# Six gate weights of the last branch staged in the pool of activations' buffers

## The chip, the cores and the metric

The kernel runs on one core of one Trainium2 chip. The metric is the device time of one execution in microseconds (us), the median of several runs.

## What is computed

A trunk of two encoder layers over 512 positions of width 1024, all in float32:

```python
h = _rms_norm(x, ln1_g[l])
proj = jnp.einsum('bsd,dn->bsn', h, w_in[l])
(a_q, a_k, a_v, b_q, b_k, b_v, c_cq, c_ckv, c_kr, gate_logits) = _split_columns(proj)
y_a = _gqa_axial(...); y_b = _diff_attention(...); y_c = _mla(...)
y = jnp.stack([y_a, y_b, y_c], axis=2)
gates = jax.nn.sigmoid(gate_logits.reshape(b, s, N_BRANCH, d))
merged = jnp.sum(gates * jnp.einsum('bsne,ned->bsnd', y, w_branch[l]), axis=2)
x = x + jnp.einsum('bsd,de->bse', merged, w_out[l])
h2 = _rms_norm(x, ln2_g[l])
x = x + jnp.einsum('bsf,fd->bsd', jnp.square(jax.nn.relu(h2 @ w_ff1[l])), w_ff2[l])
```

Three attentions with 8 heads each (A, B, C) run from the same normalised input. Each is projected to width 1024 and weighted by its own gate. The change touches the gate of the third branch, C (the latent attention).

## The kernel before

**Weights.** Each weight is loaded as a raw float32 tile `wr` by a DMA that SP's queue issues, and is then split into two parts for TensorE: ACT copies it to a rounded `wh` (line 61), and POOL (in the attention stages) or DVE (elsewhere, gate 7 included) takes the rest into `wl` (line 67). POOL does this in pieces of 256 columns. A matmul of a weight against a split activation is three matmuls per block of 128 rows: `wh` against the high part, `wh` against the low part, `wl` against the high part. The raw tiles share one pool tag, "wr", of only two buffers; `wh` and `wl` have three each. A raw buffer is free again when both `wh` and `wl` have been made from it.

**Activations.** Nearly all activations (queries `c_Q`, keys `c_K`, values, outputs `ya`/`yb`/`yc`, gate values `gc`) are tiles of 4 KB per partition and share another tag, "s4", of 25 buffers. A raw gate weight, 128 x 1024 float32, has the same size.

**Order.** A plan lists steps with estimated costs. `weave` mixes the steps of an attention (scores of a head and a block of 128 queries) with fill steps (projections, gates). Fetches and splits are called some microseconds of planned time ahead of their step. The framework's scheduler then takes every instruction with its place in that order as priority, hands out pool buffers as they come free, and writes the final order of each engine's instructions; each engine works through its own list in order and waits where an instruction isn't ready. So a pool that has a free buffer earlier or later changes the order on all engines.

**The stage.** Attention C of a layer runs with these fills: with heads 4 and 5, the last query and key projection `c_pair(l, 3)` and gates 0 to 2 of branch C; with heads 6 and 7, gates 3 to 5; after it, gates 6 and 7 and then the eight branch projections `br`. One gate is 24 matmuls (8 blocks of 3). Per unit of attention, PE does scores `sc` (3 matmuls into one of two banks of PSUM), DVE a maximum `mx`, ACT the exponential `p` (line 602), DVE the normalisation `p` (line 607), PE four transposes `pT` (line 613), ACT and DVE the split `pt` (lines 616, 617), and PE for each pair of units eight matmuls `pv`. `c_pair` gives two queries (`c_Q`, lines 228 and 233) and two keys (`c_K`), each finished by copies that SP's queue issues (line 238). The final part of a head goes by `fx`, `yt` and `yc` (lines 626, 627, 228).

**Names.** Of layer 0, the raw tiles of the eight gates of branch C are, in order, `wr_5501`, `wr_5652`, `wr_5728`, `wr_5814`, `wr_5914`, `wr_6007` (the six of the change, called gate 0 to 5 here) and `wr_6091`, `wr_6120` (gates 6 and 7). The tiles split from gates 0, 1 and 2 are `wh_5565`, `wh_5654`, `wh_5730`. Layer 1 has the same rows under other numbers.

Of the kernel before, what the change touches and what calls it, by code (L numbers as in the profile page):

```python
# [10 lines left out]
F32 = mybir.dt.float32  # L11
# [31 lines left out]
class Weight:  # L43
# [5 lines left out]
    def fetch(self):  # L49
        if self.raw is None:  # L50
            t = self.t
            self.raw = t.p.tile([128, self.cols], F32, tag=self.tag, name="wr", bufs=t.NWR if self.tag == "wr" else 4)
            t.nc.sync.dma_start(self.raw, self.src)

    def get(self):
# [86 lines left out]
class Trunk:  # L142
# [836 lines left out]
    def gate_branch(self, l, n, d):  # L979

        nc = self.nc
        wg = self.big(l, P_GATE + n * 8 + d)
        wb = self.big(l, P_BR + n * 4 + d // 2, (d % 2) * 512, 512)
        st = {}

        def gate():
            ps = self.ps("L", "gate")
            self.mm(ps, self.fm_pairs(wg, 0, self.xg))
            if n < 2:
                t = self.tmp("gz")  # L990
            else:
                if d % 2 == 0:
                    self.gc[d // 2] = self.s4("gc", dtype=F32)
                t = self.gc[d // 2][:, d % 2]
            st["t"] = t
            nc.vector.tensor_tensor(t, ps, self.rbc, op=ALU.mult)
            nc.scalar.activation(t, t, AF.Tanh, scale=0.5)

        def branch():
            t = st["t"]  # L1000
            ps = self.ps("L", "br")
            self.mm(ps, self.fm_pairs(wb, 0, [self.want(self.ys["abc"[n]], j) for j in range(4)]))
            if n == 0:
                if d % 2 == 0:
                    self.mg[d // 2] = self.s4("mg", dtype=F32)
                nc.vector.scalar_tensor_tensor(self.mg[d // 2][:, d % 2], t, 1.0, ps, op0=ALU.add, op1=ALU.mult)
            else:
                nc.vector.scalar_tensor_tensor(t, t, 1.0, ps, op0=ALU.add, op1=ALU.mult)
                m = self.mg[d // 2][:, d % 2]
                (self.pool if n == 1 else nc.vector.tensor_tensor)(m, m, t, op=ALU.add)  # L1010
                if n == 2:
                    self.mp[d] = self.s4("mp")
                    self.split(self.mp[d], m, 0.5)

        return [(24 * 0.216, gate, [wg]), (12 * 0.216, branch, [wb])]
# [373 lines left out]
```

## Time and profile before

| | |
|---|---|
| time, median of 3 runs | 1870.81 us (1870.26 to 1872.25) |
| profiled execution, its own time | 1866.2 us |
| span of that execution, first to last instruction | 1864.4 us |
| PE busy | 1817.5 us, 97% of the span |
| PE weight loads, beside it | 1599.2 us, 86% |
| DVE busy | 1371.9 us, 74% |
| ACT busy | 1005.0 us, 54% |
| POOL busy | 458.9 us, 25% |
| mean granted TensorE clock | 0.996 |

An engine's busy time over the span says how much room the others have. PE is idle for 46.9 us of the span. Timeline rows give the start, the duration, engine, line and operation, the tiles (out <- in, without buffer numbers), and in brackets how long the engine stood idle ahead of it and what released it. The stage of the change lies at about 434 to 523 us in layer 0 and 919.7 us later in layer 1.

### The profile page before, as it was taken

The numbers are of one execution on the slowest core, as the hardware profiler recorded it, in microseconds if no ns is written. First come the engines' busy times: TensorE is split into PE (matmuls) and PEld (weight loads), VectorE is DVE, ScalarE is ACT, GpSimd is POOL, SyncE is SP. The second block draws the span as 40 slices with busy tenths as digits, with TensorE's granted clock in tenths as the row PEclk, the third lists the DMA queues.
The fourth block names the chain that finished last, engine by engine and source line by source line (L and its number), as shares of the span: only waits on it lengthen the run. The fifth ranks groups of instructions, "written<-read, shape, count | busy, mean of one in ns | idle before, by whom it ended". The sixth has DMA issues, their size and how long they took to land.

```text
span 1864.4 us, 30102 instructions
## 1 busy us (share of the span) xinstructions
PE 1817.5 (97%) x10960; PEld 1599.2 (86%) x10960; DVE 1371.9 (74%) x2812; ACT 1005.0 (54%) x1844; POOL 458.9 (25%) x602
## 2 busy tenths in 40 slices
PE   7999999999999999999999999999999999999997
PEld 7998878787888898988999988787878888989897
DVE  7788889755665776767887888896566667777677
ACT  5477666655543544444445766665554444444443
POOL 4321443454101010101232224434540001001011
PEclk9999999999999999999999999999999999999999
DMA  5413341332153373645534134313232435637363
GB/s 164 115 51 85 97 109 48 97 84 81 52 170 102 92 178 107 156 130 128 153 114 122 41 92 120 90 49 87 81 93 65 168 91 121 166 92 190 102 146 95
DMA packets 87619, 201.45 MB, mean 108 GB/s; under 512 B 12464, under 2 KB 29232, under 8 KB 87472
## 3 DMA queue, kind: packets, MB, share of 16 engines
q1 hardware_dynamic: 77104, 182.75, 33.3%
q0 software_dynamic: 10368, 16.78, 5.9%
q8 instruction: 87, 1.43, 0.3%
q14 instruction: 60, 0.49, 0.1%
HBM read 174.32 MB, written 4.19 MB: 96 GB/s over the span
## 4 chain that ended last, share of the span: by engine, by line
PE 77%; DVE 10%; DMA 5%; ACT 4%; issue 2%; POOL 2%; SPq 0%; DVEq 0%; ACTq 0%; POOLq 0%
PE ff L225 17%; PE ff L1165 13%; PE gate L225 12%; PE br L225 6%; PE tm L317 6%; PE out L225 5%; PE sc L225 4%; PE pv L225 4%; PE pT L613 4%; PE c_rank L225 2%; DMA fa<-wff 2%; DMA fs<-wff 1%; DMA wr<-w 1%; DVE mx L597 1%; DVE p L759 1%
## 5 line engine op out<-in xcount | busy, mean ns | idle before, releaser
L61 ACT CAST wh<-wr 128x1024 fp32r<-128x1024 f32 (+5 forms) x246 | 224.7, 914 | 348.2 <-PE ff L225 114.0
L67 POOL TENSOR_TENSOR wl<-wr,wh 128x256 fp32r<-128x256 f32 (+1 forms) x382 | 281.3, 766 | 513.6 <-ACT wh L61 496.7
L1165 PE MATMUL ff<-h,fh 128*128 128x256 f32 x1792 | 324.6, 284 | 1.5 <-DVE x L1173 1.4
L225 PE MATMUL ff<-xg,wh 128*128 128x512 f32 x1024 | 315.8, 390 | 0.0
L1165 PEld LDWEIGHTS ff<-h,fh 128*128 128x128 f32 x1792 | 278.8, 192 | 3.7 <-issue 2.0
L1165 PE MATMUL ff<-h,fl 128*128 128x256 f32 x896 | 254.1, 285 | 2.3 <-DVE fl L116 2.0
L225 PE MATMUL gate<-xg,wh 128*128 128x512 f32 x768 | 241.9, 393 | 1.1 <-DVE c_K L233 1.1
L225 PEld LDWEIGHTS ff<-xg,wh 128*128 128x128 f32 x1024 | 191.7, 188 | 39.3
L115 ACT CAST fh<-fa 128x640 fp32r<-128x640 f32 (+1 forms) x144 | 108.7, 762 | 178.6 <-PE ff L1165 92.5
L317 PE MATMUL tm<-wh,xg 128*128 128x256 f32 x1024 | 203.0, 290 | 0.0
L597 DVE TENSOR_REDUCE mx<-sc 128x1 f32<-128x512 f32 x256 | 173.6, 683 | 35.2 <-PE sc L225 34.2
L225 PE MATMUL ff<-xg,wl 128*128 128x512 f32 x512 | 199.2, 389 | 0.0
L1165 PEld LDWEIGHTS ff<-h,fl 128*128 128x128 f32 x896 | 171.0, 192 | 5.8 <-DVE fl L116 5.3
L225 PEld LDWEIGHTS gate<-xg,wh 128*128 128x128 f32 x768 | 143.1, 189 | 29.9 <-PE pv L225 1.4
L317 PEld LDWEIGHTS tm<-wh,xg 128*128 128x128 f32 x1024 | 165.1, 192 | 0.2
L67 DVE TENSOR_TENSOR wl<-wr,wh 128x1024 fp32r<-128x1024 f32 (+3 forms) x122 | 140.1, 1149 | 25.5 <-ACT wh L61 25.4
L116 DVE TENSOR_TENSOR fl<-fa,fh 128x640 fp32r<-128x640 f32 (+1 forms) x144 | 126.2, 880 | 38.4 <-ACT fh L115 35.2
L225 PE MATMUL gate<-xg,wl 128*128 128x512 f32 x384 | 150.6, 392 | 0.0
L616 ACT CAST pt<-pT 128x512 fp32r<-128x512 f32 x192 | 111.8, 585 | 65.0 <-PE pT L613 63.5
L617 DVE TENSOR_TENSOR pt<-pT,pt 128x512 fp32r<-128x512 f32 x192 | 131.2, 685 | 19.5 <-ACT pt L616 18.1
L317 PE MATMUL tm<-wl,xg 128*128 128x256 f32 x512 | 145.4, 284 | 0.0
L613 PE MATMUL pT<-ident,p 128*128 128x128 f32 x768 | 115.8, 274 | 11.0 <-DVE p L607 5.4
(253 smaller groups left out, 3491.2 us busy)
## 6 DMA issues: line engine op xcount, KB each, us to landing
wr<-w SPq DMA_DIRECT2D x170, 512.0 KB, 3.6
fa<-wff SPq DMA_DIRECT2D x64, 320.0 KB, 3.5
wr<-w SPq DMA_DIRECT2D x52, 256.0 KB, 2.9
fa<-wff SPq DMA_DIRECT2D x32, 384.0 KB, 3.8
b_sq<-b_f SPq DMA_DIRECT2D x96, 64.0 KB, 2.7
b_sk<-b_f SPq DMA_DIRECT2D x96, 64.0 KB, 2.0
fa<-wff POOLq DMA_DIRECT2D x16, 320.0 KB, 5.2
fs<-wff SPq DMA_DIRECT2D x32, 160.0 KB, 2.8
```

Of the source, the lines that this page charges most:

```text
L61: t.nc.scalar.copy(wh, self.raw)
L67: e.tensor_tensor(wl[:, q], self.raw[:, q], wh[:, q].bitcast(F32), op=ALU.subtract)
L115: t.nc.scalar.copy(a, x)
L116: t.nc.vector.tensor_tensor(b, x, a.bitcast(F32), op=ALU.subtract)
L225: self.nc.tensor.matmul(out, l, r, start=(i == 0), stop=(i == n - 1))
L317: self.nc.tensor.matmul(ps, l, r, start=(u == 0 and i == 0 and tt % 2 == 0), stop=(u == 1 and tt % 2 == 1 and i == len(p) - 1))
L597: nc.vector.tensor_reduce(m, s, axis=AX.X, op=ALU.max, negate=True)
L613: nc.tensor.transpose(T[:, k], p[:, k * 128 : (k + 1) * 128], self.ident)
L616: nc.scalar.copy(h[:, :, q], T)
L617: nc.vector.tensor_tensor(lo[:, :, q], T, h[:, :, q].bitcast(F32), op=ALU.subtract)
L759: nc.vector.scalar_tensor_tensor(p0, p1, z1, p0, op0=ALU.mult, op1=ALU.add)
L1165: nc.tensor.matmul(bk[tag], x, y, start=(new and a == 0), stop=(part[1] == n and a == len(pairs) - 1), skip_group_check=True)
```

## The change

The raw tiles of gates 0 to 5 of branch C (`n == 2 and d < 6`) carry the tag "s4" in place of "wr", so they come out of the 25 buffers of activations. The number of "s4" buffers stays 25.

```diff
@@ class Weight, fetch @@
-            self.raw = t.p.tile([128, self.cols], F32, tag=self.tag, name="wr", bufs=t.NWR if self.tag == "wr" else 4)
+            self.raw = t.p.tile([128, self.cols], F32, tag=self.tag, name="wr", bufs={"wr": t.NWR, "s4": t.NS4, "pt": 4}[self.tag])
@@ Trunk.gate_branch @@
         wg = self.big(l, P_GATE + n * 8 + d)
+        if n == 2 and d < 6:
+
+            wg.tag = "s4"
         wb = self.big(l, P_BR + n * 4 + d // 2, (d % 2) * 512, 512)
```

Instructions, tiles and bytes are the same in both kernels; only their order and their buffers differ, and only in this stage, in both layers alike. SP's queue before, from the raw tile of gate 0 on (`c_Q_5537`, `c_Q_5543` are the last two queries, `c_K_5579`, `c_K_5584` the last two keys):

```order
L53 DMA wr_5501<-w1024 128x1024
L53 DMA wr_5652<-w1024 128x1024
L238 DMA c_Q_5537<-c_qr_4395 32x512 x2
L53 DMA wr_5728<-w1024 128x1024
L238 DMA c_Q_5543<-c_qr_4395 32x512 x2
L53 DMA wr_5814<-w1024 128x1024
L238 DMA c_K_5579<-c_krf_3505 64x512
L238 DMA c_K_5584<-c_krf_3505 64x512
L53 DMA wr_5914<-w1024 128x1024
L53 DMA wr_6007<-w1024 128x1024
L53 DMA wr_6091<-w1024 128x1024
L53 DMA wr_6120<-w1024 128x1024
```

The same place of SP's queue in the changed kernel:

```order
L53 DMA wr_6091<-w1024 128x1024
L53 DMA wr_6120<-w1024 128x1024
L53 DMA wr_5501<-w1024 128x1024
L238 DMA c_Q_5537<-c_qr_4395 32x512 x2
L238 DMA c_Q_5543<-c_qr_4395 32x512 x2
L238 DMA c_K_5579<-c_krf_3505 64x512
L238 DMA c_K_5584<-c_krf_3505 64x512
L53 DMA wr_5652<-w1024 128x1024
L53 DMA wr_5728<-w1024 128x1024
L53 DMA wr_5814<-w1024 128x1024
L53 DMA wr_5914<-w1024 128x1024
L53 DMA wr_6007<-w1024 128x1024
```

Gates 6 and 7 now take the two "wr" buffers first and keep them; gate 0's raw tile stands third, in the buffer (and with the wait: the scores `sc_5471`) that `c_Q_5537` had before; the copies of `c_Q` and `c_K` are no longer parted by weights; and gates 1 to 5 come behind them. Gate 1's raw tile takes the buffer of gate 0's, once that has been split. The others take buffers that this stage's `c_pair` leaves.

ACT's list before, from the cast of gate 0 on:

```order
L61 CAST wh_5565<-wr_5501 128x1024
L616 CAST pt_5453<-pT_5520 128x4x128
L602 ACTIVATE p_5514,z_5515<-sc_5508,mx_5512,c_rq_4065 128x512
L61 CAST wh_5654<-wr_5652 128x1024
L228 ACTIVATE c_Q_5537<-uq_5527 64x512 x2
L602 ACTIVATE p_5559,z_5560<-sc_5553,mx_5557,c_rq_4065 128x512
L61 CAST wh_5730<-wr_5728 128x1024
L228 ACTIVATE c_Q_5543<-uq_5527 64x512 x2
L228 ACTIVATE c_K_5579<-uk_5572 64x512 x2
L616 CAST pt_5589<-pT_5591 128x4x128
L602 ACTIVATE p_5604,z_5605<-sc_5598,mx_5602,c_rq_4065 128x512
L228 ACTIVATE c_K_5584<-uk_5572 64x512 x2
```

ACT's list in the changed kernel, from the third row of that piece on:

```order
L602 ACTIVATE p_5514,z_5515<-sc_5508,mx_5512,c_rq_4065 128x512
L228 ACTIVATE c_Q_5537<-uq_5527 64x512 x2
L228 ACTIVATE c_Q_5543<-uq_5527 64x512 x2
L602 ACTIVATE p_5559,z_5560<-sc_5553,mx_5557,c_rq_4065 128x512
L228 ACTIVATE c_K_5579<-uk_5572 64x512 x2
L616 CAST pt_5589<-pT_5591 128x4x128
L602 ACTIVATE p_5604,z_5605<-sc_5598,mx_5602,c_rq_4065 128x512
L228 ACTIVATE c_K_5584<-uk_5572 64x512 x2
L626 COPY fx_5618<-pv_5462 64x512
L228 ACTIVATE yc_5621<-yt_5370 128x512
L616 CAST pt_5589<-pT_5661 128x4x128
L1000 ACTIVATE gc_5649<-gc_5649 128x512
```

The casts of gates 1 and 2 (`wh_5654`, `wh_5730`) have left this piece; they now stand three and five rows behind its end. The cast of gate 0 stays where it was.

On PE the piece between gate 0 and gate 1, as a difference (unmarked and "+" rows are the changed kernel's):

```order
 L225 MATMUL sc<-c_K,c_Q 128x512 x2
 L225 MATMUL sc<-krl,c_Q 128x512
+L225 MATMUL pv<-pt,c_V 128x256 x8
+L225 MATMUL sc<-c_K,c_Q 128x512 x2
+L225 MATMUL sc<-krl,c_Q 128x512
+L613 MATMUL pT<-ident,p 128x128 x3
 L225 MATMUL gate<-xg_97,wh 128x512 x2
 L225 MATMUL gate<-xg_97,wl 128x512
```

Before, gate 1 followed the scores `sc_5677` and `sc_5689` at once; now `pv_5744`, the scores `sc_5762` and three transposes of `p_5683` (the exponential of `sc_5677`) stand ahead of it. Ahead of gate 3 the eight matmuls `pv_5930`, and ahead of gate 5 one `pv`, have moved up in the same way.

## The prediction

> **What bounds the kernel now.** I read the page's head, then TensorE's waits in the two stretches that the change touches, then the engines' rows in order of time there.
>
> ```profile
> span 1864.4 us, 30102 instructions
> PE 1817.5 (97%) x10960; PEld 1599.2 (86%) x10960; DVE 1371.9 (74%) x2812; ACT 1005.0 (54%) x1844; POOL 458.9 (25%) x602
> ```
>
> PE is the bound: a change that leaves its instructions alone can gain only from its idle time, 46.9 us in all. The waits of PE from 440 to 530 us (columns: who waited for whom, total, times, longest) are one row, and from 1360 to 1450 us, the same stage in layer 1, the answer is the same row:
>
> ```profile
> PE pT L613 <- DVE p L607: 2.5, 1, 2.5
> ```
>
> So at stake here is one stall per layer. Around it, PE's rows (start, duration; the last is layer 1's):
>
> ```profile
> 449.06 0.60 PE L613 MATMUL pT<-ident,p 128*128 128x128 f32 x4
> ...
> 450.19 1.08 PE L225 MATMUL pv<-pt,c_V 128*128 128x256 f32 x8
> 451.11 0.63 PE L225 MATMUL gate<-xg,wh 128*128 128x512 f32 x2
> ...
> 456.57 0.60 PE L613 MATMUL pT<-ident,p 128*128 128x128 f32 x4
> 459.65 0.63 PE L613 MATMUL pT<-ident,p 128*128 128x128 f32 x4 [2.49 <-DVE p L607]
> ...
> 1379.29 0.63 PE L613 MATMUL pT<-ident,p 128*128 128x128 f32 x4 [2.45 <-DVE p L607]
> ```
>
> After gate 0 (451.11 to 456.57) PE waits for the normalised `p_5604`. ACT's rows say why, with the last SP row of a weight ahead of them and its landing:
>
> ```profile
> 441.28 1.18 SPq L238 DMA_DIRECT2D c_Q<-c_qr  x2
> 449.41 0.33 SPq L53 DMA_DIRECT2D wr<-w  x1
> DMA to landing us min/median/max: 4.5/4.5/4.5
> 443.83 1.05 ACT L61 CAST wh<-wr 128x1024 fp32r<-128x1024 f32 x1 [0.22 <-issue]
> 445.14 0.59 ACT L616 CAST pt<-pT 128x512 fp32r<-128x512 f32 x1 [0.26 <-PE pT L613]
> 445.81 0.78 ACT L602 ACTIVATE p<-sc,mx,c_rq 128x512 f32<-128x512 f32 x1
> ...
> 448.07 1.07 ACT L228 ACTIVATE c_Q<-uq 64x512 fp32r<-64x512 f32 x2
> 449.03 0.76 ACT L602 ACTIVATE p<-sc,mx,c_rq 128x512 f32<-128x512 f32 x1
> ...
> 454.04 1.05 ACT L61 CAST wh<-wr 128x1024 fp32r<-128x1024 f32 x1 [4.15 <-DMA wr<-w]
> 455.12 1.08 ACT L228 ACTIVATE c_Q<-uq 64x512 fp32r<-64x512 f32 x2
> 456.22 1.19 ACT L228 ACTIVATE c_K<-uk 64x512 fp32r<-64x512 f32 x2
> 457.44 0.58 ACT L616 CAST pt<-pT 128x512 fp32r<-128x512 f32 x1
> 457.92 0.78 ACT L602 ACTIVATE p<-sc,mx,c_rq 128x512 f32<-128x512 f32 x1
> ...
> 460.04 0.58 ACT L626 COPY fx<-pv 64x512 f32<-64x512 f32 x1
> 461.38 0.63 ACT L228 ACTIVATE yc<-yt 128x512 fp32r<-128x512 f32 x1 [0.76 <-DVE yt L627]
> ```
>
> ACT stands 4.15 us before the cast of gate 2's raw tile: issued at 449.41, when a "wr" buffer came free, it lands 4.5 us later. Behind that cast wait `c_Q`, `c_K` and the exponential (457.92) that PE's transposes at 459.65 need. After that stall the granted clock (second column from the right but one) falls in layer 0, and doesn't in layer 1:
>
> ```profile
> 460.00:462.00 2.00, 2.00 (x9) 1.59 (x8) 1.92 (x3) 1.21 (x4) 0.00 (x0) 0.63 0.42 170
> 462.00:464.00 2.00, 2.00 (x7) 1.54 (x5) 1.35 (x4) 2.00 (x5) 0.98 (x2) 0.51 0.00 0
> 1380.00:1382.00 2.00, 2.00 (x10) 1.66 (x9) 1.97 (x4) 1.24 (x3) 0.00 (x0) 1.00 0.29 117
> ```
>
> The clock there is 0.63 and 0.51 of full speed: 2 x 0.37 + 2 x 0.49 = 1.7 us lost in layer 0, none in layer 1.
>
> **Removed.** With the casts of gates 1 and 2 out of this piece of ACT's list, the 4.15 us wait is gone, and with it the stalls: -2.49 - 2.45 = -4.9 us. The clock loss of 1.7 us goes with the long gap: -1.7 us.
>
> **Added: gate 0's raw tile comes later.** It was in place when its cast ran at 443.83. Now it is issued where the `c_Q` copies stood, at 441.28. I take 4.5 us to land, the row of the raw tile at 449.41, since that one too had two `c_Q` copies behind it: 445.8. The raw tile of gate 7 is in flight 0.9 us ahead of it. Bounds: 3.6 us (the same size without company, first row below) and 7.9 us (the last of four of this size issued within 2 us, second row).
>
> ```profile
> wr<-w SPq DMA_DIRECT2D x170, 512.0 KB, 3.6
> DMA to landing us min/median/max: 5.0/6.7/7.9
> ```
>
> So ACT's list shifts by 445.85 - 443.83 = 2.0 us at this cast. `p_5514`, two rows on, feeds the transposes at 449.06. Cast to cast start takes 0.95, `pt` 0.48 more: exponential at 447.3 (before: 445.81); from its start to the end of the normalisation takes 1.6 (rows below), 448.9: just in time, cost 0 to 0.3, taken as 0.1.
>
> The nearest unhindered passage from scores to a normalised `p` (PE, DVE, ACT, DVE):
>
> ```profile
> 483.67 0.39 PE L225 MATMUL sc<-krl,c_Q 128*128 128x512 f32 x1
> 484.10 0.69 DVE L597 TENSOR_REDUCE mx<-sc 128x1 f32<-128x512 f32 x1 [0.33 <-PE sc L225]
> 485.08 0.78 ACT L602 ACTIVATE p<-sc,mx,c_rq 128x512 f32<-128x512 f32 x1 [1.18 <-DVE mx L601]
> 486.18 0.48 DVE L607 TENSOR_SCALAR p<-p,z 128x512 f32<-128x512 f32 x1
> ```
>
> From the start of an exponential to the end of its normalisation 486.66 - 485.08 = 1.6; to the end of the exponential 0.8.
>
> **Added: a chain on ACT that ends late.** From `p_5514` (447.3 to 448.15) the list reads, with the durations above: `c_Q` pair 1.07; then DVE's normalisation, maximum and `c_Q` remainder, on which the second pair waits, 0.9; `c_Q` pair 1.07; exponential 0.9; `c_K` pair 1.2; `pt` 0.5; exponential 0.9; `c_K` pair 1.2; `fx` 0.6; DVE's `yt` 0.8; `yc` 0.6. Sum 9.7: `yc` ends at 457.9 (before: 462.0). The two exponentials in it are normalised by 453.3 and 455.3, ahead of the transposes at 456.57 and 457.0. Hence PE runs on without the stall: transposes to 457.45, scores `sc_5677` and `sc_5689` to 458.8. There stands now `pv_5744`, not gate 1. Its second matmul needs DVE's `pt`, which comes after `yc`'s remainder and gate 0's product, three DVE operations of 0.6 from start to start (each 0.7 long) from 457.9: 459.75. PE waits 0.9, and `pv` ends at 460.6. Next `sc_5762` needs its PSUM bank back from `p_5683`: behind that `pt` come DVE's maximum, one more `pt` and a small scaling, 1.4, exponential from 461.2 to 462.0: PE waits 1.4. The transposes wait for the normalisation (462.8, PE is there at 462.65): 0.15. Gate 1's cast is done at 463.1; its third matmul waits for POOL's first piece:
>
> ```profile
> 463.02 2.83 POOL L67 TENSOR_TENSOR wl<-wr,wh 128x256 fp32r<-128x256 f32 x4 [5.05 <-ACT wh L61]
> 488.01 2.82 POOL L67 TENSOR_TENSOR wl<-wr,wh 128x256 fp32r<-128x256 f32 x4 [6.81 <-ACT wh L61]
> ```
>
> A piece is 0.7 and two matmuls cover 0.45: 0.25. Together 2.7 per layer. Ahead of gate 3 and gate 5 the same kind of tight passage costs about 0.2 (the scores amid gate 3 for their bank) and 0.15 (`yt` ahead of `pv`): 0.35. Per layer 0.1 + 2.7 + 0.35 = 3.15; both layers +6.3.
>
> Bounds of this term: below, with ACT and DVE never late, the scores chain alone is left: `mx` start to exponential end is 485.86 - 484.10 = 1.8 and 0.2 from the scores, against 1.6 of PE work (`sc_5689`, `pv`), 0.35, with 0.1 and 0.25 as above: 0.7 per layer. Above, a landing of 7.9 shifts the whole chain by 3.4: 6.5 per layer.
>
> **Costed at nothing.** The copies of `c_Q` and `c_K` keep SP's queue from gate 1 for some 4 us, but gate 1's raw tile waits for POOL to finish gate 0 (about 450) anyway, and five raw tiles at even 2 us each are there before their casts, the first at 462. Gates 6 and 7 hold both "wr" buffers until their casts, near 500 to 505 where POOL's last piece ended at 490.8 before; behind them wait the raw tiles of the branch projections. Their cover:
>
> ```profile
> 523.22 22.09 PE br L225 x96
> wr<-w SPq DMA_DIRECT2D x52, 256.0 KB, 2.9
> ```
>
> The first of them needs 2.9 to land and two passes of 0.7 before 523.2, so there are over 10 us to spare; if that cover were gone, PE would wait at `br`. POOL, at 25%, has one piece of gate 0 moved behind two additions, done before gate 0 starts.
>
> **Sum.** -4.9 - 1.7 + 6.3 = -0.3 us on the profiled execution: 1866.2 goes to 1865.9. That execution was 4.6 us faster than the median of the runs shown, 1870.81, so against the runs I forecast 1870.5: no change that can be told, for about 0.2% (3.7 us, 1867.1 to 1874.5) is what a measurement of this kernel resolves. Its own range, the landing moved by half a microsecond either way and the clock loss kept or not, is 1868 to 1874.
>
> **The rivals.**
> *The cover holds (faster).* If gate 0 lands in 3.6 us, or ACT and DVE interleave better than I chain them, 0.7 per layer is left: 1.4 - 4.9 - 1.7 = -5.2, 1865.6. For it: nothing in the list is blocked by a load any more. Against: each of the eleven links from 447.3 on is a measured duration, with no slack put in.
> *The late raw tile (slower).* Gate 0's cast now heads ACT's list with a load issued only 2.5 us before its turn. Each microsecond of later landing is one per layer. From 2.0 us more than taken (6.5) the kernel is slower by over 0.2%; at 7.9 it is -0.3 + 2 x 3.4 = +6.5: 1877.3. For it: gate 7's raw tile and four copies share the engines. Against: at 449.41 such company cost 0.9.
> *The clock.* In layer 0 a gap of 2.49 us cost 1.7 us of clock, in layer 1 one of 2.45 cost none. If the gaps of 0.9 and 1.4, 0.9 us apart, lower it in both layers, it is -0.3 + 3.4 = +3.1: 1873.9. Against: in the rows above only the single long gap did it, and once of two.
> On this the Trainium skill, TensorE: Matmul & The Clock Gate, says in "Part 1: The HAM clock gate (the "warmup" mystery)" that the clock halves after an idle window of about 3.4 us, free-running, so that it varies from run to run; by that alone neither gap would count, and here a gap of 2.49 did, while the half speed and its irregularity agree. The same page of the Trainium skill, in "A second HAM failure mode: psum-queue depth-cycling", says that frequent small idles between groups of matmuls also make it swing; that speaks against this change and is this rival.
> *Nothing gained, nothing new.* PE's order is changed but the one wait only renamed: 1870.8.
>
> **How the numbers follow.** New short waits eat the old one, as summed: 0.45. Cover holds: 0.27. Clock: 0.12, half of it over the bound of 0.2%, of which it falls short by 0.6 us. Late raw tile: 0.13. Nothing: 0.03. Faster 0.27; slower 0.13 + 0.06 = 0.19; same 0.54. The range, 1865.5 to 1875.5, takes in the forecast's own, the rival below to its value, the clock's, and the late tile's nearer part; what lies outside is about 0.17.
>
> **What would show it.** Right: no wait of `pT` for `p` of 2.5 us near 457 and 1377; ACT's wait for a raw tile about 2.0 at 443.8, none of 4.15 at 450; new waits of PE for `pt` (0.9) and of `sc` for `p` on ACT (1.4) near 459 to 462; gate 2's start within 0.5 us of 1390 in layer 1. Wrong: a landing far from 4.5, `sc` or `pT` waiting at 449, `br` waiting at 523, or a clock below 0.9 after the small gaps. What would make the prediction wrong most easily is the DVE order around `yc`, where four operations queue in front of the `pt` that PE needs.

## The result, and the profile after

| | before | changed |
|---|---|---|
| time, median | 1870.53 us (1868.88 to 1872.25, 6 runs) | 1880.98 us (1878.96 to 1884.15, 6 runs) |
| ratio to before | | 1.0063, 95% interval 1.0053 to 1.0073 |
| span of the profiled execution | 1864.4 us | 1877.8 us |
| `uq` to the first `br`, layer 0 | 390.13 to 523.06: 132.9 us | 389.90 to 527.15: 137.3 us |
| `uq` to the first `br`, layer 1 | 1309.75 to 1441.35: 131.6 us | 1312.86 to 1452.13: 139.3 us |

The changed kernel is slower by 0.63%, 11.8 us by that ratio (the two medians differ by 10.5); forecast were 1870.5 us and no change. The two stages are 4.3 and 7.7 us longer in the profile, 12.0 of the 13.4 us between the two profiled spans: the loss lies in them. The changed kernel's page begins:

```profile
span 1877.8 us, 30092 instructions
PE 1819.8 (97%) x10960; PEld 1598.8 (85%) x10960; DVE 1373.5 (73%) x2812; ACT 1002.8 (53%) x1844; POOL 464.4 (25%) x602
```

PE works about as long as before (1817.5) and waits longer. Its waits in the two stretches where before had one row each (440 to 530 us, then 1360 to 1460 us):

```profile
PE pT L613 <- DVE pt L617: 2.7, 1, 2.7
PE pT L613 <- DVE p L607: 2.2, 1, 2.2
PE sc L225 <- ACT p L602: 0.9, 1, 0.9
PE pv L225 <- DVE yt L627: 0.2, 1, 0.2
...
PE pT L613 <- DVE pt L617: 3.4, 1, 3.4
PE pT L613 <- DVE p L607: 2.0, 1, 2.0
PE sc L225 <- ACT p L602: 1.2, 1, 1.2
PE pv L225 <- DVE pt L617: 0.9, 1, 0.9
PE pv L225 <- DVE yt L627: 0.2, 1, 0.2
```

The row of before, `pT` for `p`, is still there, at another place: ahead of gate 0 instead of behind it. And there is a row that the prediction did not have at all, `pT` for `pt`, the largest of each list. Each has its own cause.

*Ahead of gate 0.* PE's row, ACT's rows up to the exponential that PE waits for, and the issue and landing of gate 0's raw tile (the last two lines; issued at 441.1):

```profile
451.14 1.04 PE L613 MATMUL pT<-ident,p 128*128 128x128 f32 x4 [2.16 <-DVE p L607]
447.48 1.05 ACT L61 CAST wh<-wr 128x1024 fp32r<-128x1024 f32 x1 [4.10 <-DMA wr<-w]
448.44 0.58 ACT L616 CAST pt<-pT 128x512 fp32r<-128x512 f32 x1
448.91 0.78 ACT L602 ACTIVATE p<-sc,mx,c_rq 128x512 f32<-128x512 f32 x1
L53 SPq DMA_DIRECT2D wr<-w x1: 328/328/328, 441.1 to 441.1; - x1
DMA to landing us min/median/max: 6.3/6.3/6.3
```

The tile is issued where the prediction put it (441.28) but needs 6.3 us, not 4.5. ACT stands 4.10 us before its cast, as long as it stood before that of gate 2's tile in the kernel before, and the exponential two rows on comes too late for PE.

*Amid gate 6.* PE, ACT, DVE, POOL and SP's queue in layer 0, with the landing of the load issued at 509.01; then ACT and PE in layer 1; last, the same cast of ACT in layer 0 of the kernel before:

```profile
510.51 0.40 PE L225 MATMUL gate<-xg,wh 128*128 128x512 f32 x1
513.62 0.66 PE L613 MATMUL pT<-ident,p 128*128 128x128 f32 x4 [2.71 <-DVE pt L617]
511.62 0.62 ACT L61 CAST wh<-wr 128x512 fp32r<-128x512 f32 x1 [3.02 <-DMA wr<-w]
512.14 0.58 ACT L616 CAST pt<-pT 128x512 fp32r<-128x512 f32 x1
512.27 0.69 DVE L67 TENSOR_TENSOR wl<-wr,wh 128x512 fp32r<-128x512 f32 x1 [2.35 <-ACT wh L61]
512.88 0.68 DVE L617 TENSOR_TENSOR pt<-pT,pt 128x512 fp32r<-128x512 f32 x1
501.49 7.50 POOL L67 TENSOR_TENSOR wl<-wr,wh 128x256 fp32r<-128x256 f32 x8 [13.19 <-ACT wh L61]
509.01 4.30 SPq L53 DMA_DIRECT2D wr<-w  x3
DMA to landing us min/median/max: 2.5/2.5/2.5
...
1435.02 0.62 ACT L61 CAST wh<-wr 128x512 fp32r<-128x512 f32 x1 [4.23 <-DMA wr<-w]
1437.02 0.66 PE L613 MATMUL pT<-ident,p 128*128 128x128 f32 x4 [3.38 <-DVE pt L617]
...
506.75 0.62 ACT L61 CAST wh<-wr 128x512 fp32r<-128x512 f32 x1 [1.15 <-issue]
```

The 128x512 cast is that of the first branch weight (`wr_6206`). Its buffer is held by gate 6's raw tile until POOL has split gates 5 and 6 (501.49 to 508.99); the load is issued at 509.01 (before: 490.9) and lands 2.5 us later. PE needs that weight only at `br`, some 15 us on. But the cast stands in ACT's list ahead of a `pt` cast that PE needs at once, and ACT, which gets there at 508.6, waits 3.02 us in front of it. In DVE's list too the weight's split (512.27) stands ahead of that `pt` (512.88). In the kernel before, the same cast ran at 506.75 without waiting for a load.

The clock (third column from the right) falls after one stall of each layer:

```profile
444.00:454.00 10.00, 7.84 (x35) 6.29 (x34) 5.39 (x11) 4.89 (x9) 4.40 (x6) 0.86 0.43 113
454.00:464.00 10.00, 9.61 (x52) 8.17 (x51) 8.54 (x18) 7.28 (x15) 0.00 (x0) 0.97 0.58 233
...
1430.00:1440.00 10.00, 6.62 (x35) 5.30 (x34) 5.73 (x11) 4.13 (x9) 2.10 (x3) 0.88 0.24 79
1440.00:1450.00 10.00, 10.00 (x49) 8.44 (x48) 2.54 (x5) 2.46 (x5) 0.00 (x0) 0.95 0.29 93
```

10 x (0.14 + 0.03) = 1.7 us lost in layer 0, as before, and 10 x (0.12 + 0.05) = 1.7 us in layer 1, where before lost none.

### The profile page after: what moved, and what is told of

Read it like the earlier page. It is cut to its first block, busy times and chain, and to the rows that moved or that the text cites. A ratio compares the mean times of both kernels' runs of the same rounds, so it can differ in the third digit from the quotient of the medians.

```text
span 1877.8 us, 30092 instructions
## 1 busy us (share of the span) xinstructions
PE 1819.8 (97%) x10960; PEld 1598.8 (85%) x10960; DVE 1373.5 (73%) x2812; ACT 1002.8 (53%) x1844; POOL 464.4 (25%) x602
## 4 chain that ended last, share of the span: by engine, by line
PE 73%; DVE 12%; DMA 6%; ACT 4%; issue 2%; POOL 2%; SPq 0%; DVEq 0%; ACTq 0%; POOLq 0%
PE ff L225 17%; PE ff L1168 13%; PE gate L225 12%; PE br L225 6%; PE out L225 5%; PE tm L317 5%; PE sc L225 4%; PE pv L225 3%; PE pT L613 3%; PE c_rank L225 2%; DMA wr<-w 2%; DMA fa<-wff 2%; DVE mx L597 1%; DMA fs<-wff 1%; DVE fl L116 1%
## 5 line engine op out<-in xcount | busy, mean ns | idle before, releaser
L67 POOL TENSOR_TENSOR wl<-wr,wh 128x256 fp32r<-128x256 f32 (+1 forms) x382 | 286.5, 780 | 536.8 <-ACT wh L61 505.5
```

Of the source, the lines that this page charges most:

```text
L67: e.tensor_tensor(wl[:, q], self.raw[:, q], wh[:, q].bitcast(F32), op=ALU.subtract)
```

## The experiments

Two theories of the loss: a late raw tile of gate 0 (A) and a late branch weight whose cast blocks ACT (B). Gate 0's tag decides A, the tags of gates 6 and 7 decide B. That gives a square of four kernels, of which the changed one is a corner: its PE, DVE and ACT lists are row for row those of "gates 1 to 5", and those of "gates 0 to 7" are row for row those of "gates 1 to 7". "Measured" is the ratio to the kernel before, run beside it on the same chip, with its 95% interval; the passage behind `>` was written before the run.

**Gates 1 to 5** (A undone).

```diff
-        if n == 2 and d < 6:
+        if n == 2 and 1 <= d < 6:
```

> Gates 1 to 5 in the pool of activations' buffers, gate 0 back in the two raw buffers. The lists of PE, DVE and ACT are row for row those of the changed kernel; only loads move: gate 0's raw tile is again the first of the raw tiles, gates 6 and 7 still stand in the raw buffers early. Two-causes theory (late gate 0 tile; late branch weight): the wait of ACT for gate 0's raw tile (4.10 us at 447.48) and with it PE's stalls of about 2.2 us at 451 and 1371 and the clock loss of 1.7 us in layer 0 go, the stalls amid gate 6 (2.7 and 3.4 us, and 1.7 us of clock in layer 1) stay: 1881.0 - 5 = 1876 (1874 to 1877.5). Rival, the late gate 0 tile is the only cause and the rest follows from it: 1869 to 1871. Rival, the order of PE's list itself costs the time: within 1.5 us of 1881.

Measured 1.0033 (1.0022 to 1.0045), within the theory's range. PE's waits, 430 to 530 us:

```profile
PE pT L613 <- DVE pt L617: 2.7, 1, 2.7
PE sc L225 <- ACT p L602: 1.2, 1, 1.2
PE pv L225 <- DVE yt L627: 0.2, 1, 0.2
```

With the same lists, the stall ahead of gate 0 is gone and the one amid gate 6 is not. That rules out both rivals: the order alone is not the loss, and B does not follow from A.

**Gates 0 to 7** (B undone).

```diff
-        if n == 2 and d < 6:
+        if n == 2:
```

> All eight gates of branch C in the pool of activations' buffers: the two raw buffers hold the first two branch weights early, gate 0's raw tile stands behind them in SP's queue and takes the buffer of an old query as in the changed kernel. Two-causes theory: the wait of ACT for the first branch weight (3.02 us at 511.62), PE's stalls amid gate 6 (2.7 and 3.4 us) and the clock loss behind the second (1.7 us) go, the stalls at 451 and 1371 stay: 1881.0 - 7.8 = 1873 (1871.5 to 1875). The raw tiles ahead of gate 0's are half as large (256 KB in place of 512), so it may land sooner than 6.3 us, which would give up to 4 us more. Rival, the late gate 0 tile is the only cause: 1880 to 1881. Rival, the order of PE's list (changed here in 12 rows, near gate 6): within 1.5 us of 1881.

Measured 1.0004 (0.9995 to 1.0012), better than the 1873 of the theory, by the reserve it named: gate 0's raw tile has loads of 256 KB ahead of it and lands in 4.6 us. PE's waits from 430 to 530 us, and issue and landing of that tile:

```profile
PE sc L225 <- ACT p L602: 1.2, 1, 1.2
PE pv L225 <- DVE pt L617: 0.9, 1, 0.9
PE pT L613 <- DVE p L607: 0.4, 1, 0.4
PE pv L225 <- DVE yt L627: 0.2, 1, 0.2
...
L53 SPq DMA_DIRECT2D wr<-w x1: 327/327/327, 442.1 to 442.1; - x1
DMA to landing us min/median/max: 4.6/4.6/4.6
```

No wait for `pt` amid gate 6. The rest is, by chance of the neighbours, the case that the prediction summed: a landing of 4.5 and 3.15 us of waits per layer, of which 0.9 for `pt` and 1.4 for `sc`. Here they are 0.9 and 1.2, and 2.7 in all.

**Gates 1 to 7** (both undone).

```diff
-        if n == 2 and d < 6:
+        if n == 2 and 1 <= d:
```

> Gates 1 to 7 in the pool of activations' buffers, gate 0 in the raw buffers: neither cause is left. The lists of PE, DVE and ACT are row for row those of the kernel with all eight gates moved. Two-causes theory, additive: 1881.0 - 5 - 7.8 = 1868 (1866 to 1870), that is 1 to 4 us faster than before, since the 2.5 us stalls of before are gone as well. Rival, the order of PE's list itself: 1879 to 1882. Rival, new short waits as the prediction summed them (2.7 us per layer at 459 to 463) stand by themselves: 1870 to 1872.

Measured 0.9987 (0.9978 to 0.9996), in the middle of the range of the two-causes theory; the third rival, from 0.9997 on, lies just outside the interval. Against gates 1 to 5 on the same chip B is 0.46%, 8.6 us, though PE's lists of these two differ in a few rows around gates 5 and 6 as well; against gates 0 to 7 a landing of 4.6 is 0.17%, 3.2 us. What the new order costs by itself is left:

```profile
PE sc L225 <- ACT p L602: 1.2, 1, 1.2
PE pv L225 <- DVE yt L627: 0.2, 1, 0.2
```

**Gate 2 only.**

```diff
-        if n == 2 and d < 6:
+        if n == 2 and d == 2:
```

> Only gate 2's raw tile, the one whose landing ACT awaited for 4.15 us before, comes from the pool of activations' buffers; gates 0, 1, 3 and 4 stay in the raw buffers, and gates 6 and 7 too, each behind an earlier gate. Theory (the 2.5 us stall of before is the load of gate 2 alone, and the loss of the changed kernel is gate 0 and the branch weights): no stall of pT for p near 457 and 1377, 1870.5 - 4.9 = 1865.6, to 1864 with the clock loss of layer 0 gone. Rival, another wait takes its place at once (p behind the copies of c_K on ACT): 1869.5 to 1871.5.

Measured 0.9963 (0.9949 to 0.9976), faster than before. PE's list is row for row that of before, PE has no wait at all in the stage in either layer, and the clock stays at 1.00. ACT goes from gate 1's cast to the exponential without a wait for a load, and the next cast of a gate (462.39) does not wait either, if not by much: the latest raw tile issued ahead of it, at 456.70, took 5.3 us and was there at 462.0. ACT's rows:

```profile
448.84 1.05 ACT L61 CAST wh<-wr 128x1024 fp32r<-128x1024 f32 x1 [0.42 <-POOL mg L243]
...
456.69 0.78 ACT L602 ACTIVATE p<-sc,mx,c_rq 128x512 f32<-128x512 f32 x1
...
462.39 1.03 ACT L61 CAST wh<-wr 128x1024 fp32r<-128x1024 f32 x1
```

So the stall of before was that one tile's, and it does not come back elsewhere.

**The changed kernel again**, beside the last three, on one chip.

> The changed kernel once more, beside the next ones on one chip. Every theory: 1.0063 times the kernel before (1.0053 to 1.0073), with the stalls of 2.2 us at 451 and 2.7 us at 514.

Measured 1.0061 (1.005 to 1.0073), with stalls of 2.5 and 2.9 us in layer 0, 2.5 and 3.2 in layer 1.

**Branches 0 to 3** (B's load kept as late, its cast moved).

```diff
         wb = self.big(l, P_BR + n * 4 + d // 2, (d % 2) * 512, 512)
+        if n == 2 and d < 4:
+            wb.tag = "s4"
```

> The changed kernel, with the raw tiles of the first four branch weights of C taken from the pool of activations' buffers too. They do not load earlier: in SP's queue they now stand behind two later branch weights that wait for the same raw buffers of gates 6 and 7, so the first is issued at about 509 or later, as in the changed kernel. But in ACT's list its cast now stands behind the pt casts of the stage, not ahead of them; nothing else in the lists of PE and ACT differs. Theory (the cast's place in ACT's list makes the late load a stall): PE's 2.7 and 3.4 us amid gate 6 go with the clock loss behind them, the late gate 0 tile stays: 1.0063 less 9 of 1870 us, ratio 1.0015 (1.0005 to 1.0025). Rival, the late load itself is the loss, and PE waits at br instead (it is issued after 509, lands 2.5 to 3 later, and needs two splits of 0.7 before br at about 524, so a wait of at most 1 to 2 us): ratio 1.004 to 1.006. Rival, POOL and DVE slow each other's splits of gates 6 and 7 and that delays PE: 1.005 to 1.0065.

Measured 1.0024 (1.0015 to 1.0033): 0.37% less than the changed kernel, within the theory's range. SP's queue of branch weights, ACT's `pt` cast, ACT's first branch casts, the first `br`, and the landing of gate 0's tile (issued at 443.5, behind two of 512 KB):

```profile
511.54 2.70 SPq L53 DMA_DIRECT2D wr<-w  x6
511.29 0.59 ACT L616 CAST pt<-pT 128x512 fp32r<-128x512 f32 x1 [0.16 <-PE pT L613]
521.18 1.13 ACT L61 CAST wh<-wr 128x512 fp32r<-128x512 f32 x2
527.31 0.63 PE L225 MATMUL br<-yc,wh 128*128 128x512 f32 x2
DMA to landing us min/median/max: 6.4/6.4/6.4
```

The branch weights are issued no sooner than in the changed kernel (68.0 us after gate 0's raw tile, against 67.9 there), and `br` runs without a wait. The lists differ in one thing more than the expectation says: four of PE's transposes per layer stand three matmuls earlier, which would bring a wait for `pt` forward and not take it away; 0.4 us of that wait is left. So it is the place of the weight's cast in ACT's list, and of its split behind that in DVE's, that made the late load a stall. On this the Trainium skill, TensorE: Matmul & The Clock Gate, "Architectural detail: the array is 16× 32×32, not 1× 128×128", says that ACT's queue is strictly first in, first out; these two kernels agree.

**Gate 1 only.**

```diff
-        if n == 2 and d < 6:
+        if n == 2 and d == 1:
```

> Only gate 1's raw tile from the pool of activations' buffers; gate 0 and gate 2 share the two raw buffers, so gate 2 loads early. ACT's list has the casts of gates 1 and 2 after the exponentials, as in the kernel with gates 1 to 7 moved, and PE's list has the order of the changed kernel behind gate 0. Theory (with neither late tile what is left is the new order, whose passages from scores to exponential leave PE 1.2 and 0.2 us per layer): as gates 1 to 7, ratio 0.9987 (0.9975 to 0.9995). Rival, any order without a late load is as good as that of gate 2 alone: 0.996 to 0.997. Rival, the branch weight comes late here too: 1.002 to 1.004.

Measured 0.9976 (0.9966 to 0.9986). PE's one wait of the stage, in both layers:

```profile
PE sc L225 <- ACT p L602: 1.2, 1, 1.2
```

Up to gate 2 it has the order of the changed kernel, and its wait of 1.2; from gate 3 on it has that of before. It lies near the theory's fast end. Whether it is worse than gate 2 alone the intervals, which overlap, don't tell; the wait does.

**Gates 2 and 4.**

```diff
-        if n == 2 and d < 6:
+        if n == 2 and d in (2, 4):
```

> Gates 2 and 4 from the pool of activations' buffers. With gate 2 alone no wait of PE was left in the stage, so there is nothing more to gain: ratio 0.9963 (0.995 to 0.9975). Rival, gates 6 and 7 come into the raw buffers earlier and hold back the branch weight as in the changed kernel: 0.998 to 1.002.

Measured 0.9951 (0.9938 to 0.9964), the lowest ratio of all, 1859.86 us. In the stage it has 0.2 us of waits per layer and so is no better there than gate 2 alone (from `uq` to `br` 128.5 against 128.7 us); the difference lies outside the stage, within the intervals.

**All in one table.** Waits of PE in the stage of each layer (us, summed from the waits of PE), clock loss (10 us times what the clock lacks of 1.00, in windows of 10 us), and their sum less the 6.6 of before, beside the measured ratio in us (times the median of before in that comparison).

| kernel | waits, layer 0 / 1 | clock loss | less before's 6.6 | measured |
|---|---|---|---|---|
| before | 2.5 / 2.5 | 1.7 | 0 | 0 |
| changed | 6.0 / 7.7 | 3.4 | +10.5 | +11.8 |
| changed again | 6.5 / 8.0 | 5.1 | +13.0 | +11.4 |
| gates 1 to 5 | 4.1 / 4.3 | 3.4 | +5.2 | +6.2 |
| branches 0 to 3 | 4.8 / 4.5 | 1.8 | +4.5 | +4.5 |
| gates 0 to 7 | 2.7 / 2.5 | 1.7 | +0.3 | +0.7 |
| gates 1 to 7 | 1.4 / 1.4 | 0 | -3.8 | -2.4 |
| gate 1 only | 1.2 / 1.2 | 0 | -4.2 | -4.5 |
| gate 2 only | 0 / 0 | 0 | -6.6 | -6.9 |
| gates 2 and 4 | 0.2 / 0.2 | 0 | -6.2 | -9.2 |

The stage's waits and the clock behind them account for every kernel within 2 us, but for the last one by 3.0. The waits and the clock are those of one profiled execution each, the measured column is of all runs.

## Why the prediction was wrong

- **Costed at nothing, the raw tiles of the branches: the step that failed.** "Over 10 us to spare" was counted from the casts of gates 6 and 7, "near 500 to 505", to `br`, the use of the weight. Both ends were wrong. A raw buffer is free only when `wl` is made too: POOL, with gates 5 and 6 to split in a row, ended at 508.99, and the load began at 509.01. And the deadline was not `br` but the weight's cast in ACT's list, ahead of a `pt` cast that PE needs at once; ACT was there at 508.6. Issued by 505 and landing in 2.5, the load would still have been in time. Price: 2.7 and 3.4 us of waits and clock loss, 8.6 us by gates 1 to 5 against gates 1 to 7, 6.9 by the changed kernel against branches 0 to 3. No rival had it.
- **Gate 0's raw tile: a term mis-sized.** 4.5 us were taken, 6.3 and (branches 0 to 3) 6.4 measured, within the bounds of 3.6 and 7.9. The row it was taken from had two small copies behind it; here a tile of its own size, issued 0.9 us earlier, was still in flight ahead of it, and six copies followed. That "such company cost 0.9" was of another company. Branches 0 to 3 against gates 0 to 7, landings of 6.4 and 4.6, give 0.0020, 3.7 us; the slope of one per layer and microsecond gives 2 x 1.8 = 3.6. The other pair, the changed kernel against gates 1 to 5 less gates 0 to 7 against gates 1 to 7, gives 0.0030 - 0.0017, 2.4 us. (The lower bound's row is the median of all 170 loads of this size, not of lone ones; the upper bound is the longest of its four, with a fifth load just ahead.)
- **Clock loss of layer 0: not removed.** It was to go with the long gap. In the profiled executions new gaps of 2.16 and 3.38 brought one in each layer.
- **The old stall, -4.9 and -1.7: rightly sized.** Gate 2 alone, where nothing takes its place, measures -6.9 us.
- **The new short waits, 3.15 per layer: nearly right.** Gates 0 to 7, whose landing is the one assumed, shows 2.7 and 2.5. The two large links are there, 0.9 for 0.9 and 1.2 for 1.4, and `yt` ahead of `pv`, 0.2 for 0.15. The transposes ahead of gate 0 waited 0.4 and 0.2 for 0.1 taken, and the small links of 0.15, 0.25 and 0.2 do not show.
- **The sum.** -0.3 with 8.6 for the branch weight and 3.7 for the landing is +12.0, with the smaller values of each, 6.9 and 2.4, +9.0; measured were +11.8 and +11.4. The late tile alone would have stayed inside the range; its end, 1875.5, was passed because the branch weight was in no case.
- **Rivals.** "Cover holds" is gates 1 to 7, with 1.4 per layer in place of 0.7. "The late raw tile" was part of the truth. "The clock" occurred in two other kernels (below), not behind the small gaps of the changed one.
- **The signs.** Two of those named for being wrong came: the landing far from 4.5, and `pT` waiting ahead of gate 0 (2.16 us). The one that stood for the branch weights, `br` waiting, stayed away while that term failed: it watched the wrong instruction.

## What to carry to other kernels

The deadline of a load is not the matmul that uses its data but the first instruction in any engine's list that waits for it, here a cast; look at what stands behind that one. And a buffer is free when its last reader is done, here POOL's split and not ACT's cast. When tiles leave a small pool, find out which later tiles move up into it and how long they hold it: here gates 6 and 7 were loaded 36 and 41 us earlier (437.0 and 440.1 in place of 472.7 and 481.2) and held back the next load by 18 us. Move the one tile that the profile names before moving its whole family: one tag gave -6.9 us, six gave +11.8.

## What the runs showed of the hardware

*Landing time follows the neighbours.* A raw tile of 512 KB landed in 3.6 us where no load was close ahead (437.0 in the changed kernel). Gate 0's tile, with the same six copies behind it each time, landed in 4.6 us behind one of 256 KB issued 0.9 us earlier (gates 0 to 7), in 6.3 and 6.4 behind one of 512 KB issued 0.9 to 1.0 us earlier.

*POOL and DVE splitting at once.* In the changed kernel POOL's eight pieces took 7.50 us, 0.94 each on average, against 0.70 before. The longest, 1.72, lay beside DVE's split of gate 7, and that split took 1.77 against 1.23:

```profile
506.39 1.72 POOL L67 TENSOR_TENSOR wl<-wr,wh 128x256 fp32r<-128x256 f32 x1
505.74 1.77 DVE L67 TENSOR_TENSOR wl<-wr,wh 128x1024 fp32r<-128x1024 f32 x1
497.16 1.23 DVE L67 TENSOR_TENSOR wl<-wr,wh 128x1024 fp32r<-128x1024 f32 x1 [0.21 <-ACT wh L61]
```

(The last row is of before.) Those 8 x 0.24 = 1.9 us may be part of the late issue at 509.01; no run separates them. The Trainium skill, GPSIMD Engine Reference, "1. Specifications", says that GpSimd and VectorE share their SBUF interface and contend when the VectorE instruction has two inputs in SBUF, as both have here; the rows agree and give a size.

*The clock.* Each loss in the stage was the same, half speed for some 3.4 us, 1.7 us lost, but whether a gap brings it varied: of six gaps of 2.7 to 3.4 us five did, of eight of 1.8 to 2.5 us three. Two gaps of 0.89 and 1.21 us, 1.1 us apart, brought it in two of six cases; so in layer 0 of gates 0 to 7, behind the second of them:

```profile
463.69 1.03 PE L225 MATMUL sc<-c_K,c_Q 128*128 128x512 f32 x2 [1.21 <-ACT p L602]
464.00:466.00 2.00, 2.00 (x7) 1.52 (x6) 1.13 (x3) 2.00 (x4) 1.35 (x2) 0.50 0.00 0
466.00:468.00 2.00, 2.00 (x7) 1.58 (x6) 1.80 (x5) 1.05 (x3) 2.00 (x4) 0.66 0.00 0
```
